# Strassen products summed inside PSUM banks, and a second up stage without GpSimd, in a two-layer diffusion backbone

## The chip, the cores and the metric

The kernel runs on one core of a Trainium2 chip as one program, written in a tile framework that orders each engine's instructions when the program is built and sets the semaphores itself. The metric is device microseconds for one execution, lower is better; three runs of a kernel give a median. The engines are TensorE (PE, with its weight loads as PEld), VectorE (DVE), ScalarE (ACT), GpSimd (POOL) and the DMA queues, here issued from SyncE (SP) and ScalarE.

## The reference, cut to what matters

Two layers work on 512 latent tokens and 256 context tokens of width 1024. Layer 1 (index 0 in the code) mixes tokens with multi-head latent attention, layer 2 (index 1) with a gated linear recurrence; each mixer is followed by a SwiGLU feed-forward block of width 2816. Only the latent tokens leave the kernel, so layer 2's feed-forward works on 512 tokens and layer 1's on all 768.

```python
def swiglu(a, w1, w3, w2):
    return (jax.nn.silu(a @ w1) * (a @ w3)) @ w2

# in each layer, after the mixer
x = x + mod_l[5] * swiglu(modulate(rms_norm(x, norm2_w[i]), mod_l[3], mod_l[4]),
                          ffn_w1[i], ffn_w3[i], ffn_w2[i])
```

All of it is float32. The kernel gets float32 accuracy by splitting each operand into a high part `hi` (rounded to the PE's fast 32-bit format, `F32R`) and the rest `lo`, and by three matmuls, hi·hi + hi·lo + lo·hi, in place of one (`mm3`).

## The kernel before

**The up stage** (`ffn`, `ffn_up`) makes g = silu(a·W1) · (a·W3) for 22 blocks of 128 features, two blocks (one pair p) at a time, p = 0 to 10. Pair 0 is done plainly (`ffn_first`). For each of pairs 1 to 10, and for each of the two matrices W1 and W3, a 2x2-block product (two feature blocks by two halves of the tokens, with the inner dimension in two halves too) is done by Strassen-Winograd with 7 block products in place of 8. A block product is `prod(t)`: 4 inner blocks by 3 matmuls, 12 matmuls of 128 x 128 weights against half of the tokens, which is 384 columns in layer 1 and 256 in layer 2. The seven token-side sums are made once, split, and kept as `ops`. One matrix of one pair is called a unit below: 7 products, 84 matmuls; a pair is two units, 168 matmuls, and a layer has 20 units.

**Weights of a unit** (`strassen_weights`, L603): two raw tiles `wf` (128x1024 each) come by DMA; DVE makes the four Strassen sums `sa`, `sb` (L611 to L615, 128x512 each); then four slots are split: j=0 is `wf` r0 (products 0 and 1), j=1 is `sa` (6 and 3), j=2 is `sb` (4 and 2), j=3 is half of `wf` r1 (5). For each slot ACT writes `sh` (a cast, L622), and the subtraction that gives `sl` (L623) is done on POOL or, for the slots in `ON_DVE`, on DVE. `ON_DVE` is empty for layer 1 and (1, 2) for layer 2. `sh` and `sl` have three buffers each, which they share with all other weights of the kernel (`wh`, `wl`, L83 and L84).

**Sums of the products** (L746 to L754): product 0 is copied from its PSUM bank to SBUF by ACT, and seven DVE additions combine the products, each reading one PSUM bank and one SBUF block `s`. Each of the seven products has a bank of its own, chosen in rotation from eight (`up_bank`: five of tag `q`, two `L`, one `M`).

**The result g** of a pair: ACT applies Silu (L687), DVE multiplies (L688). For the first `KEEP[l]` pairs (1 in layer 1, 6 in layer 2) g is split at once into `gk` (ACT cast L628, DVE subtraction L629) and stays in SBUF in both parts. The others are written to DRAM (`gd`) from the SP queue.

**The down stage** (`ffn_down`, L758) reads the `gd` pairs back through the ACT queue, splits them into `gs` (ACT L628, DVE L629), and multiplies with W2. In layer 2 it runs over 8 output blocks c; each takes 22 inner blocks by 3 matmuls of 512 columns, in the order of the pairs, with three W2 tiles per block, which ACT (L83) and POOL (L84) split. The pools of the up stage are closed before it, and `gs` lies in memory that they held.

Who runs what and in which order on an engine is fixed when the program is built: the framework takes the ready instruction of highest priority by its own estimate of times, and priority follows the order of the program text except where `at(...)` names one; none of the names in the functions below has one. Each engine then runs its list in order.

Of the kernel before, what the change touches and what calls it, by code (L numbers as in the profile page):

```python
# [17 lines left out]
P = 128  # L18
# [26 lines left out]
ADA_HEAD = ((), (16,), (20,), (), (24,), (28,), (32, 36), (48, 52, 56, 60))  # L45
ADA_HG = ((), (), (), (), (), (), (), (24, 28, 32))
ADA_O = (36,)
KEEP, SB, GSB = (1, 6), (4, 4), (7, 5)
ON_DVE = ((), (1, 2))
LAG = 6  # L50
PRIO = {"hg_head": 1000, "ada_m": -500, "ada_n": -300}
RB = BT * 320
# [3 lines left out]
class Kernel:  # L56
# [33 lines left out]
    def fetch(self, *key):  # L90
        self.ahead[key] = self.weight(*key)

    def mm3(self, out, terms):

        nc, n = self.nc, len(terms)
        for i, ((lh, ll), (rh, rl)) in enumerate(terms):
            nc.tensor.matmul(out, lhsT=lh, rhs=rh, start=(i == 0), stop=False)  # L97
            nc.tensor.matmul(out, lhsT=lh, rhs=rl, start=False, stop=False)  # L98
            nc.tensor.matmul(out, lhsT=ll, rhs=rh, start=False, stop=(i == n - 1))  # L99

    def mm3m(self, outs):

# [528 lines left out]
    def ffn(self, es, l, x, segs, acc, ps, spool=None, acc1=None):  # L631
        nc, a = self.nc, self.a
        n = segs[-1][2]
        hn = n // 2
        KP = KD // 2
        keep = KEEP[l]
        dram = self.pool(es, "gd", space=bass.MemoryType.DRAM)
        gd = [dram.tile([P, 2, n], F32, name=f"gd{p}") for p in range(keep, KF // 2)]
        kept = self.pool(es, "gk")
        gk = []  # L640
        self.norm_scale(l, 1)
        with ExitStack() as es2:
            fs = self.pool(es2, "fs")
            fop = self.pool(es2, "fop")

            ops = [fop.tile([P, 2, 7, hn], F32R, name=f"op{j}") for j in range(KP)]
            ft = self.pool(es2, "ft")
            st = lambda: ft.tile([P, 4, hn], F32, tag="s", name="s", bufs=SB[l])
            for m in ("W1", "W3"):
                self.fetch(m, (l, 0), 0, 1024)  # L650
            rbs = self.norm_rb(acc, segs, fs, lambda i, c0, c1: self.bank(ps)[:, :c1 - c0], lambda: self.bank(ps))
            sc = self.nsc[(l, 1)]

            T1 = kept.tile([P, 2, 2, n], F32, tag="g0", name="T1", bufs=1)
            T1 = T1.rearrange("p a b c -> p (a b c)")[:, :KP * hn].rearrange("p (j c) -> p j c", j=KP)
            ys, los = [], []
            for j in range(KP):
                y = None
                for i, k in enumerate((j, j + KP)):
                    y = y or st()  # L660
                    y2 = y.rearrange("p a b -> p (a b)").rearrange("p (a b) -> p a b", a=2)
                    t = y2[:, i]
                    for (s, c0, c1), rb in zip(segs, rbs):
                        with self.tc.issue_after(los[-LAG].ins) if len(los) >= LAG else nullcontext():
                            nc.vector.scalar_tensor_tensor(t[:, c0:c1], x[s][:, k, c0 - SEGS[s][1]:c1 - SEGS[s][1]], sc[:, k, s:s + 1], rb,
                                                           op0=ALU.mult, op1=ALU.mult)
                        nc.scalar.activation(y2[:, i, c0:c1], t[:, c0:c1], AF.Identity, bias=self.mod[l][:, 24 + k, s:s + 1])
                    for b in range(2):
                        o = ops[j][:, :, (0, 3, 1, 2)[2 * i + b], :]
                        los.append(self.split(o[:, 0], o[:, 1], y[:, 2 * i + b, :], nc.vector))  # L670
                ys.append(y)
            for j, y in enumerate(ys):
                with self.at("f_T"):
                    self.strassen_tokens(y, T1[:, j, :])
                    self.split(*(ops[j][:, q, 4:7, :].rearrange("p a b -> p (a b)") for q in range(2)),
                               y[:, 1:4, :].rearrange("p a b -> p (a b)"), nc.vector)
            for u in range(40, 48, 4):
                with self.at("ada_f"):
                    self.ada(l, u, 4, fs, self.big)
            for p in range(KF // 2):  # L680
                s, g = (self.ffn_first if p == 0 else self.ffn_up)(l, p, hn, ops, fs, ps, st)
                if p == 0:
                    for j, op in enumerate(ops):
                        self.split(op[:, 0, 3, :], op[:, 1, 3, :], T1[:, j, :], nc.vector)
                s, g = (t.rearrange("p a b -> p (a b)") for t in (s, g))
                with self.at("f_g"):
                    nc.scalar.activation(s, s, AF.Silu)  # L687
                    nc.vector.tensor_mul(g, g, s)  # L688
                    if p < keep:
                        gk.append(kept.tile([P, 2, 2, n], F32R, tag=f"g{p}", name="gk", bufs=1))  # L690
                        self.split(*(gk[p][:, i].rearrange("p a b -> p (a b)") for i in range(2)), g, nc.vector)
                    else:
                        nc.sync.dma_start(out=gd[p - keep], in_=g.rearrange("p (a b) -> p a b", a=2))
        with ExitStack() as es2:
            self.ffn_down(es2, l, x, segs, n, gk, gd, ps, spool, acc1)
# [30 lines left out]
    def ffn_up(self, l, p, hn, ops, fs, ps, st):  # L726
        nc = self.nc
        cs = []
        for m in ("W1", "W3"):
            raw = []  # L730
            for i in range(2):
                w = self.ring.tile([P, RING], F32, tag="wf", name="wf", bufs=4)
                nc.sync.dma_start(out=w, in_=self.a[m][l, 2 * p + i])
                raw.append(w)
            c = st()
            ws = self.strassen_weights(raw, 512, fs, ON_DVE[l])

            def prod(t):
                wh, wl = next(ws)
                o = self.up_bank(ps, hn)  # L740
                self.mm3(o, [((wh[:, k * P:(k + 1) * P], wl[:, k * P:(k + 1) * P]), (op[:, 0, t, :], op[:, 1, t, :]))
                             for k, op in enumerate(ops)])
                return o

            add = nc.vector.tensor_add
            nc.scalar.copy(c[:, 3, :], prod(0))  # L746
            add(c[:, 0, :], c[:, 3, :], prod(1))
            add(c[:, 1, :], c[:, 3, :], prod(6))
            p5 = prod(3)
            add(c[:, 2, :], c[:, 1, :], prod(4))  # L750
            add(c[:, 3, :], c[:, 2, :], p5)
            add(c[:, 1, :], c[:, 1, :], p5)
            add(c[:, 1, :], c[:, 1, :], prod(2))
            add(c[:, 2, :], c[:, 2, :], prod(5))  # L754
            cs.append(c)
        return cs

    def ffn_down(self, es, l, x, segs, n, gk, gd, ps, spool, acc):  # L758
        nc = self.nc
        gp = self.pool(es, "gp")  # L760
        chunks = ((0, 5), (5, 11)) if l == 0 else ((0, 11),)
        keep = len(gk)
        for p0, p1 in chunks:
            terms_g = []
            for p in range(p0, p1):
                if p < keep:
                    gs = gk[p]
                else:
                    with self.at("d_g"):
                        g = gp.tile([P, 2, n], F32, tag="g", name="g", bufs=2)  # L770
                        nc.scalar.dma_start(out=g, in_=gd[p - keep])
                        gs = gp.tile([P, 2, 2, n], F32R, tag="gs", name="gs", bufs=GSB[l])
                        self.split(gs[:, 0], gs[:, 1], g, nc.vector)
                terms_g += [(gs[:, 0, i, :], gs[:, 1, i, :]) for i in range(2)]
            last = p1 == KF // 2
            k0, k1 = 2 * p0, 2 * p1
            step = -(-(k1 - k0) // (-(-(k1 - k0) // 8)))
            for c in range(KD):
                terms = []
                for k in range(k0, k1, step):  # L780
                    m = min(step, k1 - k)
                    wh, wl = self.weight("W2", (l, c), k * P, (k + m) * P)
                    terms += [((wh[:, i * P:(i + 1) * P], wl[:, i * P:(i + 1) * P]), terms_g[k - k0 + i]) for i in range(m)]
                with self.at("d_mm"):
                    sg = SEGS if l == 0 else SEGS[:1] if c < KD - 1 else HALF
                    po = self.proj_out(ps, terms, sg)
                    self.residual(x, c, po, self.mod[l][:, 40 + c, :], sg, spool if last else None, acc if last else None)
                if last and l == 1:
                    nc.sync.dma_start(out=self.out[:, c, :], in_=x[0][:, c, :])
# [323 lines left out]
```

## Time and profile before

| | |
|---|---|
| median of 3 runs | 1865.28 us (1865.24 to 1866.44) |
| the profiled execution's own time | 1871.02 us |
| its span, first to last instruction | 1869.2 us |
| PE busy | 1762.3 us, 94% of the span |
| DVE, ACT, POOL busy | 1120.9, 718.9, 844.1 us |
| mean granted TensorE clock | 0.985 |

The span is cut by the profile into 40 slices of about 46.7 us. A matmul's record is longer than the spacing at which matmuls follow each other, since they are pipelined, so the busy share of PE is read together with the count of matmuls in a stretch. Layer 1's up stage runs from about 500 to 809 us, its down stage to about 1005 us; layer 2's up stage from about 1516 to 1744 us, its down stage to the end.

### The profile page before, as it was taken

What the parts mean: (1) busy time and instruction counts of PE and PEld (TensorE: products, weight loads), DVE (VectorE), ACT (ScalarE), POOL (GpSimd) and SP (SyncE); (2) the same over time, 40 slices, a digit from 0 to 9 for tenths busy, and PEclk for the clock granted to TensorE, in tenths of its full rate; (3) what the DMA queues carried; (4) which work ended last, traced back from release to release, by engine and by line L of the source; (5) the groups of instructions that cost most, each with busy time, mean ns of one, the idle gap of its engine ahead of it and who ended that gap; (6) DMA issues with size and microseconds to landing.
All of it is one profiled execution on the core that took longest, in us unless ns stands there. A gap on an engine that the chain in (4) does not pass through costs nothing. (4 is left out here: it accounts for less than half of the span.)

```text
span 1869.2 us, 33246 instructions
## 1 busy us (share of the span) xinstructions
PE 1762.3 (94%) x13708; PEld 1590.5 (85%) x13708; DVE 1120.9 (60%) x1726; ACT 718.9 (38%) x1347; POOL 844.1 (45%) x568
## 2 busy tenths in 40 slices
PE   5979999989899999999999999999998889999999
PEld 3868988778799999988887888888886689889888
DVE  5567887732777776741205666566663389999500
ACT  4445656532643333331214333333232364444311
POOL 2343342315666666643443664555442554333542
PEclk9999999999999999999999999999998999999999
DMA  8311032623222232353223211111125422233541
GB/s 286 115 63 60 20 108 97 212 84 116 76 85 100 89 111 85 100 187 100 85 76 138 69 58 58 57 48 56 47 79 180 152 73 94 92 112 113 187 126 49
DMA packets 56454, 188.84 MB, mean 101 GB/s; under 512 B 6384, under 2 KB 8688, under 8 KB 56304
## 3 DMA queue, kind: packets, MB, share of 16 engines
q1 hardware_dynamic: 54144, 176.24, 28.7%
q10 hardware_dynamic: 2160, 10.49, 1.6%
q8 instruction: 108, 1.77, 0.4%
q14 instruction: 42, 0.34, 0.1%
HBM read 174.12 MB, written 12.58 MB: 100 GB/s over the span
## 5 line engine op out<-in xcount | busy, mean ns | idle before, releaser
L84 POOL TENSOR_TENSOR wl<-wf,wh 128x1024 fp32r<-128x1024 f32 (+2 forms) x130 | 291.1, 2244 | 235.4 <-ACT wh L83 228.9
L623 POOL TENSOR_TENSOR sl<-wf,sh 128x1024 fp32r<-128x1024 f32 x80 | 163.5, 2048 | 206.1 <-ACT sh L622 206.1
L99 PE MATMUL q<-op,sl 128*128 128x384 f32 (+1 forms) x700 | 215.6, 312 | 8.9 <-DVE sl L623 5.6
L97 PE MATMUL q<-op,sh 128*128 128x384 f32 (+1 forms) x700 | 216.4, 310 | 0.7 <-ACT sh L622 0.7
L98 PE MATMUL q<-op,sh 128*128 128x384 f32 (+1 forms) x700 | 216.3, 310 | 0.0
L83 ACT CAST wh<-wf 128x1024 fp32r<-128x1024 f32 (+2 forms) x130 | 122.6, 947 | 221.6 <-PE L L98 81.0
L99 PEld LDWEIGHTS q<-op,sl 128*128 128x128 f32 x700 | 130.8, 188 | 12.4 <-DVE sl L623 8.2
L97 PEld LDWEIGHTS q<-op,sh 128*128 128x128 f32 x700 | 131.6, 188 | 1.1 <-ACT sh L622 1.1
L98 PEld LDWEIGHTS q<-op,sh 128*128 128x128 f32 x700 | 131.6, 188 | 0.0
L622 ACT CAST sh<-wf 128x1024 fp32r<-128x1024 f32 x80 | 66.9, 836 | 114.0 <-PE q L98 66.4
L1044 DVE TENSOR_TENSOR X<-X,T 128x512 f32<-128x512 f32 x96 | 75.2, 825 | 53.4 <-PE lv L969 47.0
L557 DVE SCALAR_TENSOR_TENSOR xl<-L,mod,xl 128x512 f32<-128x512 f32 x25 | 18.7, 750 | 145.3 <-PE L L99 140.7
L99 PE MATMUL L<-op,sl 128*128 128x256 f32 (+1 forms) x284 | 88.7, 312 | 1.8 <-DVE sl L623 1.7
L97 PE MATMUL L<-op,sh 128*128 128x256 f32 (+1 forms) x284 | 88.0, 310 | 0.7 <-ACT sh L622 0.7
L98 PE MATMUL L<-op,sh 128*128 128x256 f32 (+1 forms) x284 | 88.0, 310 | 0.0
L959 POOL TENSOR_SCALAR km<-X 128x512 f32<-128x512 f32 x40 | 29.7, 744 | 123.1 <-DVE X L1044 80.6
L97 PE MATMUL L<-f_hi,wh 128*128 128x512 f32 (+1 forms) x232 | 79.5, 343 | 0.0
L98 PE MATMUL L<-f_lo,wh 128*128 128x512 f32 (+1 forms) x232 | 79.4, 342 | 0.0
L99 PE MATMUL L<-f_hi,wl 128*128 128x512 f32 (+1 forms) x232 | 78.9, 340 | 0.0
L611 DVE TENSOR_TENSOR sa<-wf 128x512 f32<-128x512 f32 x40 | 73.8, 1845 | 6.9 <-POOL sl L623 6.9
L622 ACT CAST sh<-sa 128x1024 fp32r<-128x1024 f32 x40 | 42.0, 1050 | 93.2 <-PE q L98 48.8
L194 POOL TENSOR_TENSOR acc<-acc,sq 128x512 f32<-128x512 f32 (+1 forms) x30 | 32.2, 1073 | 93.8 <-ACT sq L190 66.3
(468 smaller groups left out, 5627.7 us busy)
## 6 DMA issues: line engine op xcount, KB each, us to landing
wf<-in_W SPq DMA_DIRECT2D x104, 512.0 KB, 3.5
adaw<-in_ADA SPq DMA_DIRECT2D x96, 512.0 KB, 4.3
wf<-in_HW SPq DMA_DIRECT2D x32, 512.0 KB, 3.5
wf<-in_W SPq DMA_DIRECT2D x24, 384.0 KB, 3.2
gd<-s SPq DMA_DIRECT2D x10, 768.0 KB, 3.2
g<-gd ACTq DMA_DIRECT2D x10, 768.0 KB, 5.4
wf<-in_W SPq DMA_DIRECT2D x16, 320.0 KB, 3.3
wf<-in_MWO SPq DMA_DIRECT2D x8, 512.0 KB, 3.9
```

Of the source, the lines that this page charges most:

```text
L83: nc.scalar.copy(hi[:, :n], w[:, :n])
L84: nc.gpsimd.tensor_sub(lo[:, :n], w[:, :n], hi[:, :n].bitcast(F32))
L97: nc.tensor.matmul(out, lhsT=lh, rhs=rh, start=(i == 0), stop=False)
L98: nc.tensor.matmul(out, lhsT=lh, rhs=rl, start=False, stop=False)
L99: nc.tensor.matmul(out, lhsT=ll, rhs=rh, start=False, stop=(i == n - 1))
L194: (eng or nc.gpsimd).tensor_add(acc[:, c0:c1], acc[:, c0:c1], sq[:, :n])
L557: nc.vector.scalar_tensor_tensor(xk, po, gate[:, s:s + 1], xk, op0=ALU.mult, op1=ALU.add)
L611: nc.vector.tensor_add(b(sa, 1), b(r1, 0), b(r1, 1))
L622: nc.scalar.copy(hi[:, :n], s)
L623: (nc.vector if j in on_dve else nc.gpsimd).tensor_sub(lo[:, :n], s, hi[:, :n].bitcast(F32))
L959: nc.gpsimd.tensor_scalar(km.rearrange("p (m b r) -> p m b r", b=2, r=L), mix, 1.0, 0.0, op0=ALU.mult, op1=ALU.add)
L1044: nc.vector.tensor_tensor(v, v, t, op=ALU.mult)
```

## The change

Three things are changed.

1. In `ffn_up` the sums 0+6 and 0+6+4, and 3+2, are no longer made by DVE from separate banks: product 6 and then product 4 go on accumulating in product 0's bank `u`, and product 2 in product 3's bank `v`. Between them ACT copies what the bank holds so far to SBUF. A unit then has four ACT copies and four DVE additions (one and seven before) and uses four banks (seven before). The order of the products and of their weights is the same. This holds in both layers.
2. In layer 2 `ON_DVE` names all four slots, so that POOL splits no weights there from pair 1 on.
3. In layer 2 all eleven pairs of g stay in SBUF (`KEEP` 11). The first two (`CUTS` 2) are split in the up stage as before; the other nine are kept as one float32 tile and split in the down stage, with nine `gs` buffers (`GSB` 9, was 5). No g goes to DRAM in layer 2. Layer 1 keeps and splits as before.

```diff
--- before.py
+++ after.py
@@ -45,8 +45,8 @@
 ADA_HEAD = ((), (16,), (20,), (), (24,), (28,), (32, 36), (48, 52, 56, 60))
 ADA_HG = ((), (), (), (), (), (), (), (24, 28, 32))
 ADA_O = (36,)
-KEEP, SB, GSB = (1, 6), (4, 4), (7, 5)
-ON_DVE = ((), (1, 2))
+KEEP, CUTS, SB, GSB = (1, 11), (1, 2), (4, 4), (7, 9)
+ON_DVE = ((), (0, 1, 2, 3))
 LAG = 6
 PRIO = {"hg_head": 1000, "ada_m": -500, "ada_n": -300}
 RB = BT * 320
@@ -90,13 +90,13 @@
     def fetch(self, *key):
         self.ahead[key] = self.weight(*key)
 
-    def mm3(self, out, terms):
+    def mm3(self, out, terms, new=True, more=False):
 
         nc, n = self.nc, len(terms)
         for i, ((lh, ll), (rh, rl)) in enumerate(terms):
-            nc.tensor.matmul(out, lhsT=lh, rhs=rh, start=(i == 0), stop=False)
-            nc.tensor.matmul(out, lhsT=lh, rhs=rl, start=False, stop=False)
-            nc.tensor.matmul(out, lhsT=ll, rhs=rh, start=False, stop=(i == n - 1))
+            nc.tensor.matmul(out, lhsT=lh, rhs=rh, start=(new and i == 0), stop=False, skip_group_check=more)
+            nc.tensor.matmul(out, lhsT=lh, rhs=rl, start=False, stop=False, skip_group_check=more)
+            nc.tensor.matmul(out, lhsT=ll, rhs=rh, start=False, stop=(i == n - 1), skip_group_check=more)
 
     def mm3m(self, outs):
 
@@ -633,7 +633,7 @@
         n = segs[-1][2]
         hn = n // 2
         KP = KD // 2
-        keep = KEEP[l]
+        keep, cuts = KEEP[l], CUTS[l]
         dram = self.pool(es, "gd", space=bass.MemoryType.DRAM)
         gd = [dram.tile([P, 2, n], F32, name=f"gd{p}") for p in range(keep, KF // 2)]
         kept = self.pool(es, "gk")
@@ -685,8 +685,12 @@
                 s, g = (t.rearrange("p a b -> p (a b)") for t in (s, g))
                 with self.at("f_g"):
                     nc.scalar.activation(s, s, AF.Silu)
+                    if cuts <= p < keep:
+                        gk.append(kept.tile([P, 2, n], F32, tag=f"g{p}", name="gk", bufs=1))
+                        nc.vector.tensor_mul(gk[p].rearrange("p a b -> p (a b)"), g, s)
+                        continue
                     nc.vector.tensor_mul(g, g, s)
-                    if p < keep:
+                    if p < cuts:
                         gk.append(kept.tile([P, 2, 2, n], F32R, tag=f"g{p}", name="gk", bufs=1))
                         self.split(*(gk[p][:, i].rearrange("p a b -> p (a b)") for i in range(2)), g, nc.vector)
                     else:
@@ -735,23 +739,32 @@
             c = st()
             ws = self.strassen_weights(raw, 512, fs, ON_DVE[l])
 
-            def prod(t):
+            def prod(t, o=None):
+
                 wh, wl = next(ws)
-                o = self.up_bank(ps, hn)
+                new = o is None
+                if new:
+                    o = self.up_bank(ps, hn)
                 self.mm3(o, [((wh[:, k * P:(k + 1) * P], wl[:, k * P:(k + 1) * P]), (op[:, 0, t, :], op[:, 1, t, :]))
-                             for k, op in enumerate(ops)])
+                             for k, op in enumerate(ops)], new, t in (0, 6, 4, 3, 2))
                 return o
 
-            add = nc.vector.tensor_add
-            nc.scalar.copy(c[:, 3, :], prod(0))
-            add(c[:, 0, :], c[:, 3, :], prod(1))
-            add(c[:, 1, :], c[:, 3, :], prod(6))
-            p5 = prod(3)
-            add(c[:, 2, :], c[:, 1, :], prod(4))
-            add(c[:, 3, :], c[:, 2, :], p5)
-            add(c[:, 1, :], c[:, 1, :], p5)
-            add(c[:, 1, :], c[:, 1, :], prod(2))
-            add(c[:, 2, :], c[:, 2, :], prod(5))
+
+            add, copy = nc.vector.tensor_add, nc.scalar.copy
+            b = [c[:, i, :] for i in range(4)]
+            u = prod(0)
+            copy(b[0], u)
+            add(b[0], b[0], prod(1))
+            prod(6, u)
+            copy(b[1], u)
+            v = prod(3)
+            copy(b[3], v)
+            prod(4, u)
+            add(b[3], b[3], u)
+            copy(b[2], u)
+            prod(2, v)
+            add(b[1], b[1], v)
+            add(b[2], b[2], prod(5))
             cs.append(c)
         return cs
 
@@ -763,12 +776,15 @@
         for p0, p1 in chunks:
             terms_g = []
             for p in range(p0, p1):
-                if p < keep:
+                if p < CUTS[l]:
                     gs = gk[p]
                 else:
                     with self.at("d_g"):
-                        g = gp.tile([P, 2, n], F32, tag="g", name="g", bufs=2)
-                        nc.scalar.dma_start(out=g, in_=gd[p - keep])
+                        if p < keep:
+                            g = gk[p]
+                        else:
+                            g = gp.tile([P, 2, n], F32, tag="g", name="g", bufs=2)
+                            nc.scalar.dma_start(out=g, in_=gd[p - keep])
                         gs = gp.tile([P, 2, 2, n], F32R, tag="gs", name="gs", bufs=GSB[l])
                         self.split(gs[:, 0], gs[:, 1], g, nc.vector)
                 terms_g += [(gs[:, 0, i, :], gs[:, 1, i, :]) for i in range(2)]
```

## Rows read from the trace of the kernel before

**Rows 1.** Stretches of both layers' up stages: busy time of each engine, with instruction counts.

```profile
core 0: us, PE busy (x) PEld busy (x) DVE busy (x) ACT busy (x) POOL busy (x), PEclk, DMA share, GB/s
600.00:700.00 100.00, 100.00 (x570) 100.00 (x570) 72.93 (x78) 33.64 (x38) 64.59 (x27) 1.00 0.31 104
1597.60:1620.40 22.80, 20.90 (x171) 20.14 (x170) 22.52 (x29) 10.04 (x14) 8.71 (x4) 1.00 0.29 93
1688.00:1710.00 22.00, 20.71 (x170) 20.10 (x170) 21.62 (x28) 9.14 (x11) 8.22 (x5) 1.00 0.36 119
```

**Rows 2.** Waits of PE from 1515 to 1745 us: us in total, times, longest.

```profile
PE q L99 <- DVE sl L623: 5.6, 10, 1.0
PE q L99 <- POOL sl L623: 3.2, 3, 1.1
...
PE L L99 <- DVE sl L623: 1.7, 4, 0.6
PE M L99 <- DVE sl L623: 1.2, 2, 1.0
PE M L99 <- POOL sl L623: 1.1, 1, 1.1
PE L L97 <- ACT sh L622: 0.7, 1, 0.7
```

**Rows 3.** Timeline of DVE, layer 2: start us, us, engine, line, operation.

```profile
1684.85 1.21 DVE L688 TENSOR_TENSOR s<-s 128x1024 f32<-128x1024 f32 x1
...
1692.29 1.22 DVE L623 TENSOR_TENSOR sl<-sa,sh 128x1024 fp32r<-128x1024 f32 x1
...
1693.75 0.69 DVE L611 TENSOR_TENSOR sa<-wf 128x512 f32<-128x512 f32 x1
...
1697.80 2.88 DVE L615 TENSOR_TENSOR sb<-wf,sa 128x512 f32<-128x512 f32 x1
1700.61 0.41 DVE L748 TENSOR_TENSOR s<-s,q 128x256 f32<-128x256 f32 x1
...
1706.87 1.21 DVE L688 TENSOR_TENSOR s<-s 128x1024 f32<-128x1024 f32 x1
```

**Rows 4.** Timeline of POOL over the same time.

```profile
1695.79 4.35 POOL L623 TENSOR_TENSOR sl<-wf,sh 128x512 fp32r<-128x512 f32 x2 [7.48 <-ACT sh L622]
```

**Rows 5.** Timeline of ACT, layer 2 from 1601 us, then layer 1 from 616 us.

```profile
1601.83 0.37 ACT L746 COPY s<-q 128x256 f32<-128x256 f32 x1 [2.03 <-PE q L99]
1604.32 1.07 ACT L687 ACTIVATE s<-s 128x1024 f32<-128x1024 f32 x1 [2.12 <-DVE s L754]
...
1606.28 1.05 ACT L622 CAST sh<-wf 128x1024 fp32r<-128x1024 f32 x1 [0.39 <-ACT sh L622]
...
617.75 1.49 ACT L687 ACTIVATE s<-s 128x1536 f32<-128x1536 f32 x1
619.39 0.48 ACT L746 COPY s<-L 128x384 f32<-128x384 f32 x1 [0.16 <-PE L L99]
```

**Rows 6.** Timeline of PE where layer 2's up stage ends and its down stage begins.

```profile
1742.92 0.28 PE L97 MATMUL q<-op,sh 128*128 128x256 f32 x1
...
1744.34 0.39 PE L97 MATMUL M<-gk,wh 128*128 128x512 f32 x1
1744.57 0.40 PE L98 MATMUL M<-gk,wh 128*128 128x512 f32 x1
...
1752.52 0.39 PE L97 MATMUL M<-gs,wh 128*128 128x512 f32 x1
```

**Rows 7.** Timelines of DVE, then POOL, at the same place.

```profile
1745.00 2.61 DVE L688 TENSOR_TENSOR s<-s 128x1024 f32<-128x1024 f32 x1
1749.84 1.23 DVE L629 TENSOR_TENSOR gs<-g,gs 128x1024 fp32r<-128x1024 f32 x1 [2.23 <-ACT gs L628]
...
1760.22 2.68 DVE L629 TENSOR_TENSOR gs<-g,gs 128x1024 fp32r<-128x1024 f32 x1 [0.67 <-ACT gs L628]
...
1744.13 5.19 POOL L84 TENSOR_TENSOR wl<-wf,wh 128x1024 fp32r<-128x1024 f32 x2 [0.40 <-ACT wh L83]
```

## Prediction

> **What bounds the kernel now.** I read the share of each engine first, then stretches of the two up stages, then the waits of PE, then the timelines of DVE, ACT and POOL where those waits end.
>
> The two up stages differ. In layer 1, 100 us hold 570 matmuls, PE is busy for all of them and DVE for 73% [rows 1]; matmuls of 384 columns then stand 100/570 = 0.175 us apart, and the waits of PE in that stage are empty. In layer 2 PE idles while DVE does not: DVE is busy 22.52 of 22.80 us and 21.62 of 22.00 us [rows 1]. So layer 1's up stage is set by PE and layer 2's by DVE.
>
> PE's own pace in layer 2: twelve matmuls, one product, run from 1742.92 to 1744.34 us, 1.42 us or 0.118 us each [rows 6]. A pair has 14 products, 19.9 us. From the g multiply of pair 7 at 1684.85 to that of pair 8 at 1706.87 us it takes 22.02 us [rows 3], 2.1 us more; the pairs that are also split take longer. What PE waits for is the low part `sl` of the weights [rows 2]: 13.5 us in 21 waits. A record lasts 0.28 us and the next could start after 0.118 [rows 6], so each wait costs about 0.16 us beyond its idle time: 13.5 + 21 x 0.16 = 16.9 us. The rest of the 2.1 us per pair is slips of about 0.1 us that no wait explains, and I leave them in.
>
> Why DVE is full: an addition of 128x512 takes 0.69 us when POOL is quiet and 2.88 us when it runs against a POOL subtraction [rows 3, 4]. A DVE addition that reads PSUM and one SBUF block takes 0.41 us [rows 3].
>
> **Part 1, layer 2's weights leave POOL.** DVE gains, per pair, two subtractions of 128x1024 (slot 0) and two of 128x512 (slot 3). It loses every stretched record. Its whole list for one pair after the change, at quiet durations: 8 Strassen sums x 0.69 = 5.5; 6 subtractions x 1.22 = 7.3; 2 half subtractions, which have no quiet row and are taken at the 0.69 of the same-sized sum, 1.4; 8 product additions x 0.41 = 3.3 (six of 14 are gone); the g multiply 1.21. Sum 18.7 us, and 19.9 us for pair 1, which still has its split (+1.23, the row of the same shape [rows 7]). Against PE's 20.3 us (19.9 and the slips) DVE is no longer the bound, but it is 92% full.
>
> So the waits of rows 2 should go. The ends: nothing comes back if DVE's order makes it late all the same; 16.9 us if all go. I take 16.5.
>
> **Part 2, accumulating in banks.** Three times in a unit PE must now wait for ACT: product 6 for the copy of `u` after product 0, product 4 for the copy after product 6, product 2 for the copy of `v` after product 3. Each time exactly one product lies between, and behind the waiting matmul all of PE stands still. ACT's copy takes 0.37 us in layer 2 and 0.48 in layer 1 [rows 5]; it starts about 0.16 us after the modelled end of the last matmul in layer 1, and that end is itself 0.28 - 0.12 = 0.16 us after the next product's start. In layer 2 an undisturbed copy is through 0.16 + 0.16 + 0.37 = 0.7 us into the covering 1.42 us: 0.7 us to spare. In layer 1 a product covers 12 x 0.175 = 2.1 us and the copy needs 0.8: 1.3 to spare. What can stand ahead of it on ACT is a cast of 1.05 us or Silu, 1.07 us (layer 2) and 1.49 us (layer 1) [rows 5]. One of them wholly ahead costs 0.3 us in layer 2, nothing to 0.2 us in layer 1. ACT has room: 10.04 us of a 22.8 us stretch [rows 1], and six more copies a pair are 2.2 us. If one copy in four of layer 2's 60 meets such an operation, that is 15 x 0.3 = 4.5 us, but half of them only in part: I take 2. Ends: 0 and, with a whole cast ahead of each, 60 x 0.3 = 18. Layer 1: 0.5, ends 0 and 60 x 0.2 = 12. The additions that DVE loses in layer 1 are worth nothing there, since PE's work hides DVE's.
>
> The Trainium skill's page "PSUM — Partial Sum Buffer", section "PSUM bank collisions raise a hardware error", has a rule against this form: two engines must not touch the same bank at once, two readers included. DVE's addition of `u` into the fourth block and ACT's copy of `u` into the third read the same bank one behind the other, so by this rule ACT can be held by a late DVE addition, with all later copies and casts behind it. No row of before shows it, because there each bank has one reading engine. By the rule the term would be larger by a DVE operation now and then, 1.22 us at most; it is one more way into the second rival below.
>
> **Part 3, g stays on chip, nine splits move.** In layer 2 five writes to DRAM on SP's queue and five reads on ACT's go. PE waited for none of them, as the waits hold no DMA [rows 2], so they are worth nothing; the SP queue, on which weight loads stand behind those writes, only gets freer. Four splits, four ACT casts and four DVE subtractions, go from the up stage to the start of the down stage; their gain is in part 1.
>
> The price is at the passage. Before, PE starts the down stage at 1744.34 us, without a gap, on `gk`, and needs the first `gs` at 1752.52, 8.2 us later [rows 6]. After, two pairs are ready, 12 matmuls x 0.227 = 2.7 us. The third pair needs a cast (1.05 us) and a subtraction (1.23 us), and mostly memory that the up stage held until its last product: 2.3 us at best, and DVE first has the last g to multiply, which took 2.61 us against POOL's W2 subtractions, 5.19 us for two [rows 7]. Then a pair costs DVE 1.23 us quiet and 2.68 against POOL [rows 7], PE 6 x 0.227 = 1.36 us. About: DVE free at +3, third pair split at +4.3, so 1.6 us late; of eight more pairs perhaps two or three are stretched by 1.45 us, and each quiet one wins 0.13 back: 1.6 + 2 x 1.45 - 0.8 = 3.7. Some of the multiply and of the splits may come ahead of the last product. I take 3.5 us. Ends: 0, and all nine stretched: the last split is done at 3 + 9 x 2.68 = 27.1 us, where an undisturbed PE wants it at 2.7 + 8 x 1.36 = 13.6, so 13.5.
>
> Here too the skill speaks: "SBUF — State Buffer", section "Who interferes with whom", says that a DVE instruction with two SBUF inputs and a POOL instruction that reads SBUF lock each other out for a whole instruction. 2.88 against 0.69 us agrees. By the lock each POOL subtraction of about 2.4 us can stretch one split, and three or four of them fall into this passage, which would make 1.6 + 4 x 1.45 - 0.5 = 6.9 in place of 3.7 us.
>
> **Sum.** -16.5 + 2 + 0.5 + 3.5 = -10.5 us on the profiled execution of 1871.02 us (span 1869.2 and 1.8 around it): 1860.5. That execution is 5.7 us above the median, 1865.28; the same difference on the median gives 1854.8, which I round to 1855.
>
> **Rivals.**
>
> *The passage eats the gain.* As above with most splits stretched, 8 to 12 us in place of 3.5: 1859 to 1863.5. For it: 2.68 beside 1.23 us [rows 7], and 8.2 us of cover cut to 2.7. Against it: POOL is only busy for some 12 us of the first two output blocks.
>
> *ACT becomes the bound by its order, and the kernel slower.* The list of ACT is fixed beforehand. If a cast that waits for a weight buffer stands ahead of a copy, PE waits for the copy and the buffer waits for PE's earlier matmuls: the copy comes only a cast (1.05 us) after the covering product, and PE loses about 1.05 + 0.37 + 0.3 = 1.7 us. Both layers have 40 units. Once per unit is 40 x 1.7 = 68 us less 13 gained; it decides from 0.42 us per unit (16.7 us less the 13 gained is +3.7). Likely size where it happens at all, once in three units: 23 us, 1875. For it: ACT waits for PE's release of buffers before most casts. Against it: copies are ready before the cast that is released by the next product.
>
> *DVE stays the bound.* DVE's 18.7 us are 92% of 20.3, and its additions wait for products in a fixed order. If 1 us per pair remains, 10 us of the 16.5 return: 1865, no measurable change, and the change would not have done what it does on paper: the stretch by POOL would have turned into DVE work of its own. Against it: records on DVE overlap by some 0.08 us, so the list is nearer 17.
>
> **How the numbers follow.** Forecast, 1849 to 1859: 0.66. Passage: 0.13. DVE bound: 0.10. ACT's order: 0.11. A measurement of this kernel tells 0.2%, 3.7 us, from no change, so faster ends at 1861.5. Faster: 0.66, 0.09 of the passage's 0.13, half of DVE's 0.10 (a remainder of 0.5 us per pair) and 0.02 of mild forms of ACT's order, 0.82. The same: 0.04 + 0.05 + 0.02 = 0.11. Slower: 0.07. The range runs from 1848 (all waits gone, 1 us lost at the passage and nothing on ACT) to 1863, the end of the passage's case; about 0.07 of ACT's order, 0.05 of DVE's and 0.03 below lie outside.
>
> **What would show it.** In the profile after: POOL quiet in layer 2's up stage; DVE's sums all near 0.69 us; PE at 20.3 to 20.6 us per pair; the waits for `sl` nearly gone and in their place short ones for the ACT copies; 2 to 6 us of PE idle in the first 15 us of layer 2's down stage, waiting for `gs`; layer 1's 570 matmuls per 100 us unchanged. Wrong would be: long PE waits for the copies in either layer, or a pair that still takes 22 us.

## The result and the profile after

The changed kernel takes 1846.53 us (median of 4, 1845.77 to 1853.65) against 1865.86 us of the kernel before on the same chip: ratio 0.9897, 95% interval [0.9876, 0.9918], which is 15 to 23 us less. It is faster, as forecast. The forecast of 10.5 us less was too small by almost half, and 1846.53 lies 1.5 us below the stated range, whose end is inside the interval. Runs of one kernel differ with the granted clock of the whole run: of the four, 1853.65 us had 0.982 and the others, 1845.77 to 1846.56 us, 0.987 to 0.991; the profile after is that of the longest.

First the windows of the profile after: busy time of each engine, 100 us of layer 1's up stage and two stretches of layer 2's, each of these two as long as one pair.

```profile
core 0: us, PE busy (x) PEld busy (x) DVE busy (x) ACT busy (x) POOL busy (x), PEclk, DMA share, GB/s
600.00:700.00 100.00, 100.00 (x571) 100.00 (x570) 48.40 (x57) 41.62 (x58) 66.70 (x28) 1.00 0.27 94
1585.00:1604.94 19.94, 19.94 (x170) 19.94 (x170) 16.90 (x26) 10.96 (x17) 0.00 (x0) 1.00 0.33 107
1645.00:1664.94 19.94, 19.94 (x171) 19.94 (x170) 16.90 (x26) 10.96 (x17) 0.00 (x0) 1.00 0.34 103
```

Against [rows 1] layer 2 has turned round: PE is busy all the time, DVE for 16.90 of 19.94 us, POOL not at all. A pair takes 19.94 us where it took 22.0 and 22.8. In layer 1 the count of matmuls per 100 us is what it was; DVE went from 73 to 48% and PE has nothing from it.

All waits of PE from 1522 to 1850 us, in the form of [rows 2] (us in total, times, longest), are one row:

```profile
PE M L98 <- DVE gs L629: 2.7, 1, 2.7
```

The 20 waits for `sl` of [rows 2] are gone and no wait for an ACT copy has come. Where layer 2's Strassen products begin, before, and then where they begin and where the next stage follows, after, from PE's timelines:

```profile
1517.62 0.38 PE L97 MATMUL L<-op,sh 128*128 128x256 f32 x1 [0.75 <-ACT sh L622]
...
1519.33 0.39 PE L97 MATMUL q<-op,sh 128*128 128x256 f32 x1 [0.25 <-ACT sh L622]
...
1724.96 0.39 PE L99 MATMUL M<-gk,wl 128*128 128x512 f32 x1
```

The stretch takes 205.6 us after; before, it ran from 1517.62 to 1744.34 [rows 6], 226.7 us. That is 21.1 us less, but 1.2 of them are not the change's. At the start of the stretch before, where the rest of pair 0 is still worked off, twelve matmuls from 1519.17 to 1521.52 follow each other at 0.213 us in place of 0.118, at a granted clock of 0.50, the lower of its two levels (1.2 GHz); in the profile after such a stretch lies ahead of the first Strassen product. The two in the windows of before and after:

```profile
1518.20:1521.60 3.40, 3.21 (x16) 3.02 (x15) 2.50 (x1) 3.30 (x5) 2.66 (x2) 0.50 0.50 154
1504.80:1510.00 5.20, 5.20 (x26) 5.20 (x26) 5.20 (x10) 3.08 (x6) 3.38 (x5) 0.50 0.01 3
```

So the change gave back about 20 us in this stage. Behind it stands the one wait. The timelines of PE, DVE and POOL at the passage to the down stage:

```profile
1727.26 0.40 PE L97 MATMUL M<-gs,wh 128*128 128x512 f32 x1
1730.31 0.50 PE L98 MATMUL M<-gs,wh 128*128 128x512 f32 x1 [2.65 <-DVE gs L629]
1730.64 0.40 PE L99 MATMUL M<-gs,wl 128*128 128x512 f32 x1
...
1726.64 2.48 DVE L690 TENSOR_TENSOR gk<-s 128x1024 f32<-128x1024 f32 x1
1729.04 10.44 DVE L629 TENSOR_TENSOR gs<-gk,gs 128x1024 fp32r<-128x1024 f32 x9
...
1721.48 6.55 POOL L84 TENSOR_TENSOR wl<-wf,wh 128x1024 fp32r<-128x1024 f32 x3 [201.25 <-ACT wh L83]
```

PE has worked through its two ready pairs (two of their twelve matmuls ran ahead, the others take 2.3 us from 1724.96 to 1727.26) when it needs the low part of the third. That part stands on DVE behind the last g multiply, which runs 2.48 us against POOL's W2 subtractions. The second matmul comes 3.05 us after the first instead of 0.227, so the passage costs 2.8 us, and 2.9 with the next matmul, which comes 0.33 us later. From then on the nine splits follow at 1.16 us each, faster than PE's 1.36 us per pair, and PE waits no more.

Both together are 20 - 2.9 = about 17 us, inside the interval of the medians; the two profiled spans differ by 1869.2 - 1851.9 = 17.3 us. The stages that the change does not touch vary from run to run by more than the rest: in a second profile of the same changed kernel layer 2's Strassen products begin at 1500.32 us in place of 1519.33. So the experiments below are read mainly by their stage: the pair in layer 2, and the gap at the passage.

### The profile page after: what moved, and what is told of

Read it like the earlier page. It is cut to its first block, busy times and chain, and to the rows that moved or that the text cites. A ratio compares the mean times of both kernels' runs of the same rounds, so it can differ in the third digit from the quotient of the medians.

```text
span 1851.9 us, 33106 instructions
## 1 busy us (share of the span) xinstructions
PE 1755.5 (95%) x13708; PEld 1591.8 (86%) x13708; DVE 1016.3 (55%) x1646; ACT 762.6 (41%) x1467; POOL 760.6 (41%) x528
## 5 line engine op out<-in xcount | busy, mean ns | idle before, releaser
L97 PE MATMUL q<-op,sh 128*128 128x384 f32 (+1 forms) x640 | 197.3, 310 | 1.0 <-ACT sh L622 1.0
L98 PE MATMUL q<-op,sh 128*128 128x384 f32 (+1 forms) x640 | 197.6, 310 | 0.0
L99 PE MATMUL q<-op,sl 128*128 128x384 f32 (+1 forms) x640 | 194.9, 310 | 0.0
L97 PEld LDWEIGHTS q<-op,sh 128*128 128x128 f32 x640 | 120.3, 188 | 1.5 <-ACT sh L622 1.5
L98 PEld LDWEIGHTS q<-op,sh 128*128 128x128 f32 x640 | 120.3, 188 | 0.0
L99 PEld LDWEIGHTS q<-op,sl 128*128 128x128 f32 x640 | 119.5, 188 | 0.0
L623 POOL TENSOR_TENSOR sl<-wf,sh 128x1024 fp32r<-128x1024 f32 (+1 forms) x40 | 88.7, 2218 | 56.4 <-ACT sh L622 56.4
L98 PE MATMUL L<-op,sh 128*128 128x256 f32 (+1 forms) x360 | 110.4, 307 | 0.0
L99 PE MATMUL L<-op,sl 128*128 128x256 f32 (+1 forms) x360 | 110.3, 306 | 0.0
L97 PE MATMUL L<-op,sh 128*128 128x256 f32 (+1 forms) x360 | 110.3, 306 | 0.0
L158 PE MATMUL L<-adaw,s 128*32 128x128 f32 x1216 | 57.1, 297 | 29.5 <-DMA adaw<-in_ADA 29.3
L622 ACT CAST sh<-sb 128x1024 fp32r<-128x1024 f32 x40 | 42.0, 1050 | 88.5 <-PE q L98 46.6
L158 PEld LDWEIGHTS L<-adaw,s 128*32 128x32 f32 x1216 | 34.8, 116 | 46.1 <-DMA adaw<-in_ADA 17.2
```

What stands on the lines that cost most here:

```text
L97: nc.tensor.matmul(out, lhsT=lh, rhs=rh, start=(new and i == 0), stop=False, skip_group_check=more)
L158: nc.tensor.matmul(rows_ps[32 * j:32 * j + 32, i * P:(i + 1) * P], lhsT=self.s32[:, k, :], rhs=w[:, k * P:(k + 1) * P], start=(k < 4), sto ...
L622: nc.scalar.copy(hi[:, :n], s)
L623: (nc.vector if j in on_dve else nc.gpsimd).tensor_sub(lo[:, :n], s, hi[:, :n].bitcast(F32))
```

## The experiments

**One part at a time.** Four kernels, on one chip with the kernel before (1868.26 us there, 13 runs).

*The sums alone.* The new `ffn_up` in both layers, with the settings of before:

```diff
-KEEP, CUTS, SB, GSB = (1, 11), (1, 2), (4, 4), (7, 9)
-ON_DVE = ((), (0, 1, 2, 3))
+KEEP, CUTS, SB, GSB = (1, 6), (1, 6), (4, 4), (7, 5)
+ON_DVE = ((), (1, 2))
```

> Only the sums in PSUM banks, in both layers; weights' low parts and the kept pairs as before. First theory: layer 2's up stage was set by DVE, which ran about 2.1 us per pair behind PE's 19.94 us, and any relief of DVE of that size gives nearly the whole gain. Six additions fewer per pair, which follow each other 0.335 us apart on DVE, are 2.0 us: 22.02 becomes 20.0 us, and the pairs that are also split 20.8 us; layer 2's up stage 226.6 becomes about 210 us, the passage to the down stage keeps no gap, the time is 1848 to 1851 us. Rival theory: the three parts share the gain about equally, since POOL's stretching of DVE records stays: 1857 to 1860 us, pairs near 21.3 us. If the accumulating products waited for ACT's copies, PE would show waits for ACT of more than 0.2 us at lines of the copies; both theories expect none.

1844.63 us (median of 4), ratio 0.9885 [0.9857, 0.9912]. The waits of PE from 1520 us to the end are an empty list: no gap at the passage either. Windows of a pair that is split and of one that is not:

```profile
1577.94:1597.88 19.94, 19.94 (x170) 19.94 (x170) 18.47 (x23) 11.76 (x18) 8.81 (x4) 1.00 0.31 107
1650.00:1669.94 19.94, 19.94 (x170) 19.94 (x169) 16.33 (x22) 11.11 (x17) 8.54 (x4) 1.00 0.42 140
```

The first theory holds, and by more than it said: the split pairs were to stay at 20.8 us and are at 19.94. POOL still works 8.5 to 8.8 us a pair, but DVE loses less by it. Its timeline there, and POOL's:

```profile
1582.07 1.56 DVE L614 TENSOR_TENSOR sb<-wf 128x512 f32<-128x512 f32 x1
1583.55 0.68 DVE L615 TENSOR_TENSOR sb<-wf,sa 128x512 f32<-128x512 f32 x1
1584.15 0.41 DVE L757 TENSOR_TENSOR s<-s,M 128x256 f32<-128x256 f32 x1
1584.49 1.21 DVE L692 TENSOR_TENSOR s<-s 128x1024 f32<-128x1024 f32 x1
...
1586.81 2.23 DVE L629 TENSOR_TENSOR gk<-s,gk 128x1024 fp32r<-128x1024 f32 x1 [0.78 <-ACT gk L628]
...
1584.84 3.12 POOL L623 TENSOR_TENSOR sl<-wf,sh 128x1024 fp32r<-128x1024 f32 x1 [1.76 <-ACT sh L622]
```

The split that took 3.4 us in the kernel before takes 2.23 here, and POOL's own subtraction, 2.55 us there, 3.12: the stretch is shared out differently, and PE waits for none of it.

*The weights on DVE alone.*

```diff
-ON_DVE = ((), (1, 2))
+ON_DVE = ((), (0, 1, 2, 3))
```

> Only the four subtractions of layer 2's weights on DVE; sums and kept pairs as before. First theory: with POOL silent, DVE's list for a pair is 14 additions at 0.335, 8 sums at 0.60, 6 subtractions at 1.14, 2 at 0.60 and the multiply at 1.14 us, 18.7 us, with the split of a kept pair 19.8: below PE's 19.94, so PE sets the stage: pairs of 19.9 to 20.1 us, the passage without a gap, the time 1845 to 1848 us, as good as the whole change. Rival theory: at full records this list is 21.1 us and more with the split, DVE stays the bound, pairs stay at 21 us or more: 1855 to 1862 us.

1848.42 us (median of 4), ratio 0.9901 [0.9873, 0.9929]. No waits of PE from 1520 us on. Again a split pair and one that is not:

```profile
1580.00:1599.94 19.94, 19.94 (x171) 19.94 (x170) 19.93 (x33) 10.38 (x13) 0.00 (x0) 1.00 0.29 103
1660.00:1679.94 19.94, 19.94 (x170) 19.94 (x170) 18.88 (x32) 9.25 (x12) 0.00 (x0) 1.00 0.36 131
```

DVE is busy 19.93 of 19.94 us in the split pair and PE still loses nothing. The first theory holds at its edge.

*Everything kept on chip, alone* (`KEEP`, `CUTS`, `GSB` and the reading from `gk` of the change, with the old sums and `ON_DVE` (1, 2)).

> Only the keeping of all pairs on chip in layer 2, two of them split in the up stage; sums and weights as before. First theory: DVE still sets the up stage; pairs 3 to 6 lose their split and go from 22.8 to 22.0 us, 3 to 4 us in all, and the passage to the down stage takes 2 to 4 us back: 1863 to 1867 us, no measurable change. Rival theory: the traffic to DRAM and the queues behind it cost something, and their going gives 4 us or more: 1861 us or less.

1870.47 us (median of 10), ratio 1.0011 [0.9992, 1.0029]. PE's waits in layer 2's feed-forward:

```profile
PE q L99 <- DVE sl L623: 7.1, 10, 1.0
PE M L98 <- DVE gs L629: 3.0, 1, 3.0
```

The split pairs of before go from 22.8 to 22.0 us, 3.2 us in all, and the passage gets its 3.0 us wait: one pays for the other, as the first theory has it, and no gain by the DRAM traffic is to be seen.

*The change without the sums* (the old additions in both layers, the other two parts as in the change).

> The change with the sums of before in both layers (seven banks, seven DVE additions, one ACT copy). First theory: DVE's list of 18.7 us fits under PE's 19.94 without the sums too: 1846 to 1849 us, pairs of 19.9 to 20.1 us in layer 2. Rival theory: the sums are needed for DVE to get out of the way, or layer 1 gains by them: 1852 us or more.

1851.64 us (median of 4), ratio 0.9918 [0.9897, 0.9939]; the median lies 2.6 us above the range of the first theory and just short of the rival's. The stage decides:

```profile
1660.00:1679.94 19.94, 19.94 (x170) 19.94 (x170) 18.67 (x32) 9.26 (x11) 0.00 (x0) 1.00 0.30 106
```

The pair is at 19.94 us without the sums too, and the wait for the first `gs` is there. So the sums are not needed where POOL is silent.

**The copies, made dearer.** Each of the three ACT copies of a unit for which PE must wait is done twice, then four times, with the same values (one run each):

```diff
-            copy(b[0], u)
+            for _ in range(2):
+                copy(b[0], u)
```

and likewise for `copy(b[1], u)` and `copy(b[3], v)`; with 4 in the second kernel.

> The change with each of the three copies of a unit for which PE waits done twice by ACT; the second overwrites the first with the same values. The prediction's arithmetic: the copies are through 0.32 + 0.37 + 0.35 = 1.04 us into a covering product of 1.42 us: no waits of PE, pairs of layer 2 stay at 19.94 to 20.0 us. Rival, by which any operation ahead of a copy delays PE: six places per pair by 0.2 us or more, 21 us per pair.

Twice, 1850.39 us: PE's only wait in layer 2 from 1520 us on is still that for the first `gs` (2.6 us), and a pair is at 19.94 us with ACT at 13.24:

```profile
1580.00:1599.94 19.94, 19.94 (x170) 19.94 (x169) 16.89 (x26) 13.24 (x23) 0.00 (x0) 1.00 0.33 107
```

> The same with four copies each. 0.32 + 4 x 0.35 = 1.72 us is more than the 1.42 + 0.12 us that PE gives in layer 2: each of the six waits of a pair should cost 0.2 us and 0.1 us more to get going again, 1.8 us, pairs of 21.5 to 22 us, if the slack is what the prediction took it to be. In layer 1 0.32 + 4 x 0.46 = 2.16 us against 2.1 + 0.18: pairs stay within 0.2 us of 29.5. If the copies have more room than that, layer 2 stays at 20 us.

Four times: 1870.96 us. Layer 2's pairs go to between 19.93 and 21.4 us, less than expected, and layer 1's to 30.1 to 32.0, much more than the 0.2 us that I allowed. But the longer waits of PE, in layer 2 from 1530 to 1743 us and then in layer 1 from 520 to 815, name another thing than the copies:

```profile
PE q L99 <- DVE sl L623: 1.2, 3, 0.5
PE L L97 <- ACT sh L622: 0.7, 1, 0.7
PE L L99 <- DVE sl L623: 0.7, 1, 0.7
...
PE q L99 <- POOL sl L623: 8.1, 10, 1.3
PE q L97 <- ACT sh L622: 1.1, 3, 0.4
```

PE waits for weights, not for a copy. One of these waits can be followed: at 1624.06 us PE waits 0.66 us for a cast that ACT began at 1622.93, behind two copies (1622.41 and 1622.67, 0.38 and 0.39 us). Why the others came late is not shown.

Why the copies have more room than the prediction gave them, PE's timeline of the changed kernel shows. Here is one unit, each line the first matmul of a block on one bank (the two `L` banks have one name here), and then ACT's three copies:

```profile
1576.64 0.28 PE L99 MATMUL q<-op,sl 128*128 128x256 f32 x1
1577.83 0.28 PE L97 MATMUL L<-op,sh 128*128 128x256 f32 x1
1579.26 0.28 PE L97 MATMUL L<-op,sh 128*128 128x256 f32 x1
1580.68 0.28 PE L97 MATMUL q<-op,sh 128*128 128x256 f32 x1
1580.92 0.28 PE L97 MATMUL L<-op,sh 128*128 128x256 f32 x1
1582.34 0.28 PE L99 MATMUL q<-op,sl 128*128 128x256 f32 x1
...
1584.00 0.28 PE L97 MATMUL L<-op,sh 128*128 128x256 f32 x1
...
1576.84 0.38 ACT L756 COPY s<-L 128x256 f32<-128x256 f32 x1
1579.46 0.37 ACT L761 COPY s<-L 128x256 f32<-128x256 f32 x1
1581.76 0.36 ACT L759 COPY s<-L 128x256 f32<-128x256 f32 x1
```

By the built program's list of PE's instructions, which names the banks, these blocks are product 1, product 3, product 6, two matmuls of product 5, product 2, the rest of product 5 and, after four matmuls of the next unit, product 4. The framework has put product 3 ahead of product 6 and product 4 last. So not one product but 22 matmuls lie between the copy after product 0 and product 6, 24 or 28 between products 6 and 4, and 14 between products 3 and 2 (once 24). The copies end at 1577.22, 1579.83 and 1582.12, which is 2.0, 1.1 and 1.9 us before the matmul that needs them; over all of layer 2 the least is 0.2 us, once.

In the kernel with two copies the list is nearly the same (again 14, 22 and 24 or 28 matmuls), so its run tests this room: it shrinks to 0.5 us at the least, and no wait comes. With four copies the framework draws up another list, with 20 to 60 matmuls between. That kernel measures what the copies cost with their new order, not a fixed slack of 0.7 us.

**The passage.** A third pair split in the up stage:

```diff
-KEEP, CUTS, SB, GSB = (1, 11), (1, 2), (4, 4), (7, 9)
+KEEP, CUTS, SB, GSB = (1, 11), (1, 3), (4, 4), (7, 8)
```

> The change with three pairs split in the up stage in place of two, and eight gs buffers. First theory: the passage cost 2.8 us because PE's cover of two pairs, 2.7 us, ended before the first gs was subtracted, which stood on DVE behind the last g multiply and that behind POOL. A third ready pair adds 6 x 0.227 = 1.4 us of cover, so a gap of 1.2 to 1.7 us is left; DVE has room for the split, since its 18.1 us of the pairs with a split stay under 19.94. Time 1 to 2 us below the whole change. Rival theory: all gs wait for memory of the last product and for ACT, and what is late moves with them: the gap stays near 2.8 us.

1845.8 us (median of 5), ratio 0.9895 [0.9868, 0.9923]. The wait shrinks more than by the cover that I added:

```profile
PE M L98 <- DVE gs L629: 0.2, 1, 0.2
```

The pairs stay at 19.94 us. The rest came from DVE's list, which the framework has drawn up anew too. Seven splits now stand ahead of the last g multiply, which had held up the first one:

```profile
1719.62 11.29 DVE L629 TENSOR_TENSOR gs<-gk,gs 128x1024 fp32r<-128x1024 f32 x7 [1.28 <-ACT gs L628]
...
1731.27 2.97 DVE L690 TENSOR_TENSOR gk<-s 128x1024 f32<-128x1024 f32 x1
```

PE's matmul that waits starts 4.2 us into the down stage (1717.71 to 1721.93), where it took 5.35 us in the whole change (1724.96 to 1730.31): 1.1 us of the 2.5 are this, the other 1.4 the cover. So the run does not show that cover alone was short. By the time this is about 2.5 us of 1846, which the medians cannot tell.

*The change without its third part* (six pairs split in the up stage, five through DRAM, sums and weights as in the change).

> The change without its third part: sums in PSUM banks and all weights of layer 2 on DVE, but six pairs split in the up stage and five through DRAM as before. First theory: PE sets layer 2's up stage (pairs of 19.94 us, DVE near 18 us of it where a pair is split) and the passage has no gap: layer 2's feed-forward 2.5 to 3 us shorter than with the whole change, equal to the sums alone. Rival theory: the third part is needed to make room on DVE or on the queues: pairs of 20.3 us or more.

1847.69 us (median of 7), ratio 0.992 [0.9892, 0.9948]. The pairs are at 19.94 us, the wait for the first `gs` is gone, but three smaller waits of 0.2 to 0.7 us, 1.3 in all, for W2's weights and one `gs` have come where the first output block passes into the second. About half of the gain that I expected is spent there, and the medians show none. Of all kernels with the copies this one has the only listed wait of PE for one of them, 0.2 us.

**Layer 1 alone, and the simplest version beside the change.** The new sums for `l == 0`, the old ones for layer 2, everything else as before:

```diff
+            if l == 0:
+                ...
+            else:
+                ...
```

> Only the sums in PSUM banks, and only in layer 1; layer 2 as before. First theory: layer 1's up stage was set by PE without waits, so its Strassen part keeps pairs of 29.5 to 29.6 us; only the passage from the plainly done first pair, which took 38.96 us to the second, may get 1.5 us shorter with another order on PE, as in the runs with the sums in both layers. Time within 2 us of before, layer 2's pairs at 22.0 and 22.8 us. Rival theory: part of the gain of the sums is in layer 1: 4 us or more.

1864.88 us (median of 10) against 1866.96: ratio 0.999 [0.997, 1.0011]. Layer 1 has 571 matmuls per 100 us, as ever:

```profile
600.00:700.00 100.00, 100.00 (x571) 100.00 (x570) 48.07 (x57) 41.94 (x58) 66.37 (x28) 1.00 0.27 95
```

The gain of the sums is in layer 2. The first pair of layer 1 is 1.5 us shorter, as expected, but not shown to be so by the order on PE: of two profiles of the sums alone one has 37.5 us there and the other 38.95, as before. Then the sums alone and the whole change once more, on the same chip:

> The sums alone, in both layers, again, beside the whole change on the same chip. First theory: both have layer 2 pairs of 19.94 us, and the sums alone have no gap at the passage to the down stage: the stretch from the end of layer 2's Strassen products to the end of the span is 2.5 to 3 us shorter than in the whole change, in the medians 0 to 4 us less. Rival theory: the whole change has something in the down stage, by the DRAM traffic that it saves, that makes up for the gap.

> The whole change again, beside the sums alone: a gap of 2.6 to 3.1 us once in the first 4 us of layer 2's down stage, pairs of 19.94 us; the median 0 to 4 us above the sums alone by the first theory, equal or below by the rival.

The sums alone: 1839.9 us (median of 4), ratio 0.986 [0.9837, 0.9882]. The whole change: 1850.01 us (median of 6), ratio 0.9898 [0.9867, 0.993]. The waits of PE from 1500 to 1850 us, the first row of the sums alone and the first of the whole change:

```profile
PE L L99 <- POOL wl L84: 0.3, 1, 0.3
...
```

```profile
PE M L98 <- DVE gs L629: 2.6, 1, 2.6
...
```

The trace shows what the theory said, 2.6 us more waiting in the whole change, and the stretch from the down stage's start to the end is 2.4 us longer. The medians lie 10 us apart, more than that, and the two intervals overlap. Part of it goes with the granted clock, 0.988 in the median of the sums alone and 0.984 in that of the whole change: at 0.984 the runs are 1845.19 us against 1849.04 and 1850.99. What is left over the 2.4 us is not explained by these stages. The simplest version, the first part alone, is by these runs at least as good as the whole change.

## Why the prediction was too small

**What bounds the kernel.** Right. Layer 2's up stage was set by DVE and its meetings with POOL, and either relief of DVE turns it over to PE: the sums alone do, the weights alone do.

**Part 1, DVE's list.** Right: 18.7 us at full records, nearer 17 with their overlap; measured 16.90. The Trainium skill's page "SBUF — State Buffer", section "Who interferes with whom", says that a DVE instruction with two SBUF inputs contends with a GpSimd instruction that reads SBUF. The trace after agrees in what it loses: with POOL silent the sums of 128x512 are at 0.68 to 0.69 us, every one.

**The size of the waits: the step that failed.** I took 16.5 us for the waits of rows 2 and left the rest as "slips of about 0.1 us that no wait explains, and I leave them in". They belong to the waits. Here are matmuls of 256 columns of the kernel before around one wait; undisturbed ones follow each other at 0.118 us:

```profile
1598.99 0.28 PE L98 MATMUL L<-op,sh 128*128 128x256 f32 x1
1600.35 0.38 PE L99 MATMUL q<-op,sl 128*128 128x256 f32 x1 [1.08 <-POOL sl L623]
1600.57 0.28 PE L97 MATMUL q<-op,sh 128*128 128x256 f32 x1
```

The matmul after the one that waited comes 0.22 us behind it, 0.10 late. So a wait of 1.08 us cost 1.36 + 0.22 - 2 x 0.118 = 1.34 us, 0.26 more than the idle time, where I had added 0.16. One of the 21 waits in rows 2 is not for `sl`: 0.7 us for `sh`, at the first Strassen matmul. That leaves 20 waits of 12.8 us, 12.8 + 20 x 0.26 = 18.0 us. Nine more halts of PE, too short for the list, cost 2.2 us by the starts of the stage's matmuls. So 20 us stood to be won and all of it came back, a pair of 19.94 us and not 20.3. The simpler reckoning stood in the prediction and was not used: a pair was 2.1 us over PE's own pace, and by [rows 1] 2.9 where it was also split; four pairs of each kind are 20 us.

**Part 2, the copies: the other step that failed.** I charged 2.5 us, on "Each time exactly one product lies between, and behind the waiting matmul all of PE stands still". In the program as built 14 to 28 matmuls lie between, since the framework put product 3 ahead of 6 and product 4 last, and the copies had 1.1 to 2.0 us to spare where I had reckoned 0.7. PE waited for no copy in either layer, not even with the copies doubled, although one of the three stands behind a cast in every unit of layer 2 (1580.81 us, 1.05 us, ahead of the copy at 1581.76).

The Trainium skill's page "PSUM — Partial Sum Buffer", section "PSUM bank collisions raise a hardware error", says that two engines must not access one bank at the same time, two readers included. From this I had drawn that a late DVE addition can hold ACT up. It did not: DVE's addition of `u` ran at 1645.64 us for 0.42, ACT's copy of it started at 1646.27, right behind ACT's cast of 1645.32, and ACT sat idle before none of these copies.

**Part 3, the passage.** Mechanism and place right: the last multiply against POOL, the third pair behind it. 3.5 us charged, 2.9 measured. I had two or three of the splits stretched; none was, at 1.21 to 1.23 us each, and POOL was through with its three W2 tiles at 1728.03 us and began the next at 1737.95, beside the last of the splits only. That the DRAM traffic was worth nothing fits the kernel with everything kept on chip, which is no faster than the one before.

With the measured terms the sum is -20 + 0 + 2.9 = -17 in place of -16.5 + 2.5 + 3.5 = -10.5; the rest of the 19.3 us between the medians is inside their interval. The range's lower end was not its own terms' either: all waits gone and 1 us lost is 1865.3 - 16.9 + 1 = 1849.4, not 1848. Of the rivals none came true; the passage took a seventh of the gain, not most of it.

## What to carry to other kernels

When a stage has one engine just over another, the distance between them is the whole prize, however much work is taken off: here 2.1 to 2.9 us per pair, and two parts that each remove that much do not add up. Price the prize by the period of the loop against the bound engine's own pace, not by adding up the waits that a list names. Before work is moved out of a stage that has just got room for it, ask what it covered: the splits had room in the up stage and cost 2.9 us at the start of the next. And what lies between two instructions is to be counted in the list that the framework builds, not in the program text.

## What the runs showed that was not expected

A wait of PE costs more than its idle time: the matmul behind the released one is late as well, 0.22 in place of 0.118 us at 256 columns (1600.35 to 1600.57) and 0.33 in place of 0.227 at 512 (1730.31 to 1730.64 above). And an engine can be busy for 19.93 of 19.94 us in a loop, as DVE is in the kernel with only the weights moved, without PE losing anything to it.
